# First FFN: plain fp32 products on unsplit weights for token tile 0, and the first block by token tile

## The chip, the cores and the metric

The kernel runs on one core of a Trainium2 chip. The metric is the device time of one execution in microseconds. The time before the change is 914.63 us, the median of three runs (914.24 to 914.75). The profile comes from a fourth execution, which took 913.31 us; its span, from the first to the last instruction, is 911.5 us.

## The reference

A decoder trunk with two layers on 256 tokens of width 1024, everything in float32. Around each attention stand two half-step SwiGLU FFNs with an inner width of 2816. The part that the change touches is the first FFN of the first layer:

```
h = h + 0.5 * swiglu(rms_norm(h, ffn1_norm[0]), ffn1_w_in[0], ffn1_w_out[0])

def swiglu(x, w_in, w_out):
    gate, up = split(x @ w_in, 2)        # w_in: 1024 x 5632
    return (silu(gate) * up) @ w_out     # w_out: 2816 x 1024
```

## The kernel before, in words

The 256 tokens are two tiles of 128 (t = 0 and 1). The contraction over 1024 is eight k of 128. TensorE (PE) multiplies a 128x128 piece of the transposed activations, which it holds, with a 128x512 piece of the weights, which streams through, into one PSUM bank of 512 columns.

**Split operands.** Nearly every product is made of three: each fp32 operand is split in two fp32r numbers, a rounded one (hi) and the rest (lo), and a step (`step`, L423) adds hi·hi, lo·hi and hi·lo into the bank. The weights arrive by DMA as fp32 in tiles called raw (1 MB, four k of 512 columns). ScalarE (ACT) casts a raw tile to w_hi (L404) and VectorE (DVE) subtracts to get w_lo (L406), in two pieces of 128x1024 per tile. The activations are split in the same way into one tile xT (written at L461 and L462).

**The first FFN's input.** x comes in four DMAs of 128x512 (hN). PE transposes each (L455, four 128x128 matrices into one bank), DVE multiplies the bank by the norm's gain in place (L1342), ACT casts and DVE subtracts. The factor of the root mean square is applied later, in the silu and in the product with up.

**The first block.** The FFN's 2816 columns are worked off in blocks. The first is a plain one of 512 columns (`plain`): two raw tiles of gate columns (i = 0 and 1, four k each) and two of up columns. Before the change it runs gate first, then up, and in each of them i = 0 for both token tiles and then i = 1 for both. So each w pair is used in one stretch and is free again. Its raw tiles come in four DMAs of 256 KB each. The next block is a narrow one of 256 columns, then come blocks with Strassen's seven products, and each block's part of the product with w_out lies between.

**What sets the order.** The code adds tasks with an assumed duration and a priority to a planner (`Plan`), which simulates the five engines and writes each engine's instructions in the order that comes out. So a change of constants or of tasks at the start can move everything behind it. Ahead of its first useful work PE runs products on a constant (tile warm, `warm_up`), whose result nobody reads; WARM sets how many.

**Buffers.** There are five raw tiles and five pairs of w tiles. A DMA for a raw tile stands in SP's queue until its predecessor in the same buffer has been split.

Of the kernel before, what the change touches and what calls it, by code (L numbers as in the profile page):

```python
# [44 lines left out]
FSUMS = 5000.0  # L45
TM = 1000.0
BOOST = 10000.0
C11 = True
RES = (True, True, True, True)
RES_SB = False  # L50
# [9 lines left out]


SB_ORDER = (("p", 0), ("s", 0), ("p", 1), ("v",), ("o", 0), ("s", 1), ("p", 2), ("o", 1), ("s", 2), ("p", 3), ("o", 2), ("s", 3), ("o", 3))
WARM = 14
NEWACC = False
QROT = False
ZQ = {(1, 0): 6, (2, 0): 7, (1, 1): 3}
# [2 lines left out]
EARLY = 300.0  # L69
X1 = 35  # L70
WAITM = 0
POSX = (-20000.0, -6000.0)
POSR = (-3000.0, -2000.0)
QORD = (('q', 0, 1), ('q', 0, 0), ('q', 1, 0), ('q', 2, 0), ('h', 0, 0), ('h', 0, 1), ('q', 1, 1), ('h', 1, 0), ('h', 1, 1), ('q', 2, 1), ('h', 2, 0), ('q', 3, 0), ('h', 2, 1), ('q', 3, 1), ('h', 3, 0), ('h', 3, 1))
OORD = [(0, range(6), (0, 1)), (1, range(6), (1,)), (0, range(6, 8), (0, 1)), (1, range(6, 8), (1,)), (1, range(8), (0,))]
# [20 lines left out]
class Buf:  # L96

    def __init__(self, make, base=()):
        self.make, self.base, self.ap_, self.all = make, list(base), None, []
        self.w, self.r = {}, {}  # L100
        self.slot = None
        self.by_halves = False

    @property
    def ap(self):
# [117 lines left out]
def kernel(  # L223
# [151 lines left out]
    def load(parts, a, b, cut=2):  # L375
        raw = RAW.get([P, a, b], F32, "raw")
        for sl, src in parts:
            ks = [(raw, i) for i in range(2)]
            if cut == 2 or len(parts) > 1:
                dma(src, lambda sl=sl: raw.ap[:, :, sl], P * a * (sl.stop - sl.start) * 4, ks, plan.pos - LOADS)  # L380
            else:
                for c in range(0, a, a // cut):
                    dma(src[:, c:c + a // cut], lambda c=c: raw.ap[:, c:c + a // cut], P * (a // cut) * b * 4,
                        [(raw, c)], plan.pos + 10 * c - 8.5e5)
        raw.ab, raw.cut = (a, b), cut
        return raw

    def flat(buf):
        return buf.ap.rearrange("p a b -> p (a b)")
# [3 lines left out]
    def split(raw, prio=None):  # L393
        prio = plan.pos - LEAD if prio is None else prio
        a, b = raw.ab
        hi, lo = WP.get([P, a, b], F32R, "w_hi"), WP.get([P, a, b], F32R, "w_lo")
        m = a * b // PIECES
        for j in range(PIECES):
            sl = slice(j * m, (j + 1) * m)
            ks = [j] if PIECES == 2 else [0, 1]  # L400
            rs = [2 * j, 2 * j + 1] if raw.cut == 4 else ks

            first = [(xh, (0, 0))] if raw.cut == 4 and j == 1 else []
            T("ACT", act(m), lambda sl=sl: ACT.copy(out=flat(hi)[:, sl], in_=flat(raw)[:, sl]),  # L404
              r=[(raw, i) for i in rs] + first, w=[(hi, i) for i in ks], prio=prio)
            T("DVE", dve(m), lambda sl=sl: DVE.tensor_sub(out=flat(lo)[:, sl], in0=flat(raw)[:, sl],  # L406
                                                          in1=flat(hi)[:, sl].bitcast(F32)),
              r=[(raw, i) for i in rs] + [(hi, i) for i in ks], w=[(lo, i) for i in ks], prio=prio)
        return hi, lo

    def weight(parts, a, b, cut=2, keep=False):
# [11 lines left out]
    def step(bank, w, kk, xk, first, last, cols_=every, piece=None):  # L423
        (sh, sl), keys = xk
        hi, lo = w
        piece = kk // 2 if piece is None else piece

        def run():
            r_h, r_l = hi.ap[:, kk, cols_], lo.ap[:, kk, cols_]
            mm(bank.ap, sh(), r_h, first, False)  # L430
            mm(bank.ap, sl(), r_h, False, False)
            mm(bank.ap, sh(), r_l, False, last)

        dense(3 * mmr(512), run, r=[(hi, piece), (lo, piece)] + keys, w=B(bank))

    def of_x(t, k):
        return ((lambda: xh.ap[:, k, ts(t)], lambda: xl.ap[:, k, ts(t)]), [(xh, (t, k // 4)), (xl, (t, k // 4))])
# [154 lines left out]
    def ffn(w_in, w_out, acc, rest, finish, kv=None, blocks=BLOCKS, roots=None, ending=False, there=False, arranged=False):  # L592
# [57 lines left out]
        def plain(n, c, by_t, cut=2):  # L650
# [29 lines left out]
            if by_t:  # L680
                for t in range(NT):
                    b = bank_()
                    for i in range(2):
                        gate(t, i, b)
                        if t == 1:
                            WP.put(*gw[i])
                    after_gate(t, b)
                    b = bank_()
                    for i in range(2):
                        up(t, i, b)  # L690
                        if t == 1:
                            WP.put(*uw[i])
                    after_up(t, b)
            else:
                for f, ws, fin in ((gate, gw, after_gate), (up, uw, after_up)):
                    bs = [bank_() for _ in range(NT)]
                    for i in range(2):
                        for t in range(NT):
                            f(t, i, bs[t])
                            if i == 1:  # L700
                                fin(t, bs[t])
                        WP.put(*ws[i])
# [134 lines left out]
        for n, kind in enumerate(blocks):  # L837
            if kind == "s":
                outs[n] = strassen(n, cols_[n], lambda: out(n - 1) if 0 < n < last else None)
            elif kind == "p":  # L840
                outs[n] = plain(n, cols_[n], n == 0 and not first, 4 if first and n == 0 else 2)
            else:
                outs[n] = narrow(n, cols_[n], n == 0 and not first)
            if n == last - 1:
# [492 lines left out]
    T("ACT", 60, lambda: nc.scalar.dma_start(out=gin, in_=ffn1_norm[0].rearrange("(j p k) -> p j k", j=2, k=4)), w=B(gc), prio=-9.5e5, lat=2500.0)  # L1337


    def first_operand(t, j, bank):  # L1340
        transposes(bank, lambda: [hN.ap[:, t, half(j)].rearrange("p (q k) -> p k q", k=4)[:, k, :] for k in range(4)], [(hN, (t, j))])
        T("DVE", dve(512), lambda: DVE.tensor_mul(  # L1342
            out=quarters(bank), in0=quarters(bank), in1=gin[:, j].unsqueeze(2).to_broadcast([P, 4, P])), r=B(gc), w=B(bank))
        part_to(bank, (xh, (t, j), lambda: xh.ap[:, 4 * j:4 * j + 4, ts(t)]), (xl, (t, j), lambda: xl.ap[:, 4 * j:4 * j + 4, ts(t)]), 512,
# [191 lines left out]
```

## Time and profile before

| what | value |
|---|---|
| median of three runs | 914.63 us |
| the profiled execution | 913.31 us |
| its span | 911.5 us |
| PE busy | 899.3 us (99%) |
| DVE busy | 818.2 us (90%) |
| ACT busy | 649.6 us (71%) |
| DMA | 214.44 MB, 235 GB/s in the mean |
| the chain that ended last | PE 81%, DVE 15% |

The page lists what each engine was busy with; the chain of waits goes back from the last instruction to whatever released it. A line of the kernel in these rows can be that of a helper: L283 is every product, L404 and L406 are every weight split. In the rows of the timeline the first number is the start and the second the time to the end of the last of the xN instructions. Matmuls overlap in these records (a 128x512 fp32r product is shown with some 390 ns, and follows its predecessor after 227 ns), so their cost is read from the starts.

### The profile page before, as it was taken

To read this page: it belongs to the slowest core of one execution; us is meant where nothing else is said; L and a number is where in the kernel's file an instruction comes from. 1 tells how busy PE (TensorE), PEld (TensorE's weight loads), DVE (VectorE), ACT (ScalarE), POOL (GpSimd) and SP (SyncE) were. 2 spreads that over 40 slices of the span, in tenths; PEclk is the share of its full clock that TensorE was granted. 3 is DMA by queue.
4 is the path that set the end of the run, shared out by engine and by line. 5 is a ranking of instruction groups with operands and counts; after the bars stand their busy time and mean duration, and the time that the engine had idled before them with its cause. 6 is when DMAs were issued, how large, how long until landed. Compare 5 with 4: busy or idle time off the path is not lost.

```text
span 911.5 us, 11855 instructions
## 1 busy us (share of the span) xinstructions
PE 899.3 (99%) x4446; PEld 743.7 (82%) x4446; DVE 818.2 (90%) x981; ACT 649.6 (71%) x925; POOL 65.5 (7%) x71
## 2 busy tenths in 40 slices
PE   9999999999999999999999999999999999999997
PEld 7888888888888878888888878888897777888886
DVE  7989999787967999999969999999689799999986
ACT  6857668677986865876778767667867677686663
POOL 1010101000000100110000101010000001010100
PEclk9999999999999999999999999999999999999999
DMA  9887999996853499999884999899853349998971
GB/s 335 311 203 216 306 268 242 311 246 186 264 184 126 106 260 284 236 280 303 251 269 135 251 279 276 256 326 234 298 180 116 94 94 273 293 258 268 335 209 47
DMA packets 107306, 214.44 MB, mean 235 GB/s; under 512 B 6256, under 2 KB 27760, under 8 KB 107248
## 3 DMA queue, kind: packets, MB, share of 16 engines
q1 hardware_dynamic: 85184, 170.49, 52.3%
q0 software_dynamic: 21648, 42.99, 27.2%
q8 instruction: 35, 0.57, 0.2%
q10 hardware_dynamic: 416, 0.20, 0.1%
q14 instruction: 23, 0.19, 0.1%
HBM read 212.62 MB, written 1.05 MB: 234 GB/s over the span
## 4 chain that ended last, share of the span: by engine, by line
PE 81%; DVE 15%; issue 2%; ACT 2%; POOL 0%; DVEq 0%; POOLq 0%; ACTq 0%
PE ps L283 77%; DVE w_lo L406 6%; PE ps L641 2%; DVE raw L575 1%; PE ps L455 1%; ACT w_hi L404 1%; DVE S_l L545 1%; DVE s L551 1%; DVE xT L462 1%; DVE w_lo L1115 1%; PE ps L1281 0%; DVE xs L1379 0%; DVE hN L532 0%; DVE aT_l L462 0%; DVE e L1273 0%
## 5 line engine op out<-in xcount | busy, mean ns | idle before, releaser
L406 DVE TENSOR_TENSOR w_lo<-raw,w_hi 128x1024 fp32r<-128x1024 f32 x432 | 509.3, 1221 | 30.3 <-ACT w_hi L404 28.5
L404 ACT CAST w_hi<-raw 128x1024 fp32r<-128x1024 f32 x432 | 430.1, 1050 | 96.7 <-DVE raw L575 41.1
L283 PE MATMUL ps<-w_hi,xT 128*128 128x512 f32 (+1 forms) x800 | 233.3, 375 | 0.0
L283 PEld LDWEIGHTS ps<-w_hi,xT 128*128 128x128 f32 x800 | 144.7, 188 | 25.9 <-DVE xT L462 0.2
L283 PE MATMUL ps<-w_lo,xT 128*128 128x512 f32 (+1 forms) x400 | 149.2, 373 | 0.3 <-DVE w_lo L406 0.3
L283 PE MATMUL ps<-w_hi,aT_h 128*128 128x512 f32 x354 | 139.9, 395 | 0.0
L283 PE MATMUL ps<-w_lo,aT_h 128*128 128x512 f32 x354 | 137.7, 389 | 0.0
L283 PE MATMUL ps<-w_hi,aT_l 128*128 128x512 f32 x354 | 137.5, 388 | 0.0
L283 PE MATMUL ps<-w_hi,S_h 128*128 128x512 f32 x320 | 126.9, 396 | 1.5 <-ACT p L735 1.5
L283 PE MATMUL ps<-w_lo,S_h 128*128 128x512 f32 x320 | 124.9, 390 | 0.3 <-DVE w_lo L406 0.3
L283 PE MATMUL ps<-w_hi,S_l 128*128 128x512 f32 x320 | 124.7, 390 | 0.0
L575 DVE TENSOR_TENSOR raw<-raw 128x1024 f32<-128x1024 f32 x78 | 93.7, 1221 | 0.2
L283 PEld LDWEIGHTS ps<-w_lo,xT 128*128 128x128 f32 x400 | 75.3, 188 | 14.4 <-DVE w_lo L406 1.1
L580 POOL DMA_DIRECT2D raw<-in_ffn_w_in_dram x38 | 48.1, 1267 | 516.8 <-DVE w_lo L406 218.0
L283 PEld LDWEIGHTS ps<-w_lo,aT_h 128*128 128x128 f32 x354 | 66.5, 188 | 13.9
L283 PEld LDWEIGHTS ps<-w_hi,aT_l 128*128 128x128 f32 x354 | 66.6, 188 | 12.9
L283 PEld LDWEIGHTS ps<-w_hi,aT_h 128*128 128x128 f32 x354 | 66.5, 188 | 12.8
L283 PEld LDWEIGHTS ps<-w_hi,S_h 128*128 128x128 f32 x320 | 60.1, 188 | 15.3 <-ACT p L735 3.0
L283 PEld LDWEIGHTS ps<-w_lo,S_h 128*128 128x128 f32 x320 | 60.1, 188 | 13.5 <-DVE w_lo L406 0.7
L283 PEld LDWEIGHTS ps<-w_hi,S_l 128*128 128x128 f32 x320 | 60.2, 188 | 11.6
L461 ACT CAST aT_h<-ps 128x512 fp32r<-128x512 f32 (+1 forms) x48 | 26.4, 549 | 55.1 <-PE ps L641 53.6
L283 PE MATMUL ps<-xT,w_hi 128*128 128x512 f32 (+1 forms) x136 | 46.8, 393 | 0.0
(176 smaller groups left out, 918.5 us busy)
## 6 DMA issues: line engine op xcount, KB each, us to landing
raw<-in_ffn_w_in_dram SPq DMA_DIRECT2D x76, 1024.0 KB, 7.8
raw<-in_ffn_w_out_dram SPq DMA_DIRECT2D x44, 1024.0 KB, 6.6
raw<-in_ffn_w_in_dram POOLq DMA_DIRECT2D x38, 1024.0 KB, 9.6
raw<-in_sb_w_qkv_dram SPq DMA_DIRECT2D x12, 1024.0 KB, 9.4
raw<-in_ffn_w_in_dram SPq DMA_DIRECT2D x16, 512.0 KB, 6.7
raw<-in_ffn_w_in_dram SPq DMA_DIRECT2D x16, 256.0 KB, 5.4
raw<-in_sb_w_o_dram SPq DMA_DIRECT2D x4, 1024.0 KB, 5.2
raw<-in_swa_w_q_dram SPq DMA_DIRECT2D x4, 1024.0 KB, 9.3
```

Source lines behind the costliest of these rows:

```text
L283: PE.matmul(ps, lhsT=lhsT, rhs=rhs, start=start, stop=stop, skip_group_check=True)
L404: T("ACT", act(m), lambda sl=sl: ACT.copy(out=flat(hi)[:, sl], in_=flat(raw)[:, sl]), r=[(raw, i) for i in rs] + first, w=[(hi, i) for i i ...
L406: T("DVE", dve(m), lambda sl=sl: DVE.tensor_sub(out=flat(lo)[:, sl], in0=flat(raw)[:, sl], in1=flat(hi)[:, sl].bitcast(F32)), r=[(raw, i) ...
L455: PE.matmul(bank.ap[:, i * P:(i + 1) * P], lhsT=s, rhs=ident, start=i == 0, stop=True, is_transpose=True, skip_group_check=True)
L461: T("ACT", act(n), lambda: ACT.copy(out=hi[2](), in_=src()), r=B(bank), w=[hi[0:2]])
L462: T("DVE", dve(n), lambda: DVE.tensor_sub(out=lo[2](), in0=src(), in1=hi[2]().bitcast(F32)), r=B(bank) + [hi[0:2]], w=[lo[0:2]])
L545: T("DVE", dve(512), lambda: DVE.tensor_sub(out=SL.ap[:, i].rearrange("p a b -> p (a b)"), in0=b.ap, in1=SH.ap[:, i].rearrange("p a b -> p ...
L551: T("DVE", dve(512), lambda: DVE.scalar_tensor_tensor(out=dst.ap, in0=x_.ap, scalar=sign, in1=y_.ap, op0=ALU.mult, op1=ALU.subtract), r=B( ...
L575: T("DVE", dve(m), lambda sl=sl: DVE.tensor_add(out=flat(dst)[:, sl], in0=flat(dst)[:, sl], in1=flat(src)[:, sl]), r=[(src, k) for k in ks ...
L580: T("POOL", 1500, lambda: nc.gpsimd.dma_start(out=dst.ap, in_=src, accum_op=ALU.add), w=[(dst, 0), (dst, 1)], prio=plan.pos - LOADS, lat=5 ...
L641: PE.transpose(out=tr.ap[:, i * P:(i + 1) * P], in_=m.ap[:, i * P:(i + 1) * P], identity=ident)
L1115: T("DVE", dve(512), lambda k=k, g_=g_: DVE.scalar_tensor_tensor(out=lo.ap[:, k], in0=raw.ap[:, k], scalar=g_(), in1=hi.ap[:, k].bitcast(F ...
```

## The change

Four edits meet in the first block of the first FFN.

1. **Plain products.** For token tile 0, the first six of the eight k of the gate columns are multiplied as fp32 with fp32, straight from the raw tile and from an unsplit copy of the activations (x_f), one product in place of three (`direct`). The other two k, and all of up, go on as split steps. Since token tile 1 still uses the split gate weights, all of the four raw tiles are split as before.
2. **By token tile.** The first block runs all of tile 0 (gate, then up), and then all of tile 1. The w pairs of the block are held until tile 1 has used them.
3. **Splits piece by piece.** The block's raw tiles are split in four pieces of 128x512 (one k, which is one DMA) rather than in two of 128x1024; a step waits for the piece of its own k. FINES and AFTER leave it at four pieces for each of the four tiles, and no piece waits for the first operand any more.
4. **x_f and fewer warm products.** For tile 0 DVE writes gain times transposed x to x_f in SBUF; ACT casts and DVE subtracts from there, and ACT copies x_f back into the bank (prio 0), where later sums read it. WARM goes from 14 to 9, that is from 40 products on the constant to 20. The planner's position for tile 1's operands (POSX) goes from -6000 to 0.

```diff
+DIRECT = 6
+FINES = (4,4,4,4)
+AFTER = 4
+FIRST_T = True
-WARM = 14
+WARM = 9
-POSX = (-20000.0, -6000.0)
+POSX = (-20000.0,0.0)
...
         raw.ab, raw.cut = (a, b), cut
+        raw.fine, raw.after = 2, {}
+        if cut == 4:
+            raw.fine = FINES[fines[0]]
+            if fines[0] == 0:
+                raw.after = {k: [(xh, (0, 0))] for k in range(AFTER, 4)}
+            fines[0] += 1
         return raw
...
+    def split_fine(raw, prio):
+        a, b = raw.ab
+        hi, lo = WP.get([P, a, b], F32R, "w_hi"), WP.get([P, a, b], F32R, "w_lo")
+        n = a // raw.fine
+        for c in range(0, a, n):
+            ks, at_ = range(c, c + n), [(buf, k) for buf in (hi,) for k in range(c, c + n)]
+            sl = slice(c * b, (c + n) * b)
+            T("ACT", act(n * b), lambda sl=sl: ACT.copy(out=flat(hi)[:, sl], in_=flat(raw)[:, sl]),
+              r=[(raw, k) for k in ks] + raw.after.get(c, []), w=[(hi, k) for k in ks], prio=prio)
+            T("DVE", dve(n * b), lambda sl=sl: DVE.tensor_sub(out=flat(lo)[:, sl], in0=flat(raw)[:, sl],
+                                                              in1=flat(hi)[:, sl].bitcast(F32)),
+              r=[(raw, k) for k in ks] + [(hi, k) for k in ks], w=[(lo, k) for k in ks], prio=prio)
+        hi.fine = lo.fine = True
+        return hi, lo
...
-        piece = kk // 2 if piece is None else piece
+        piece = kk if hi.fine else kk // 2 if piece is None else piece
...
+    def direct(bank, raw, kk, xf, first, last):
+        def run():
+            mm(bank.ap, xf.ap[:, kk], raw.ap[:, kk], first, last)
+
+        dense(4 * 512 / 2.4 + 20, run, r=[(raw, kk), (xf, 0)], w=B(bank))
...
                     for i in range(2):
+                        if first and t == 0 and 4 * i < DIRECT:
+                            raw = load([(slice(0, 512), col(0, i, c))], 4, 512, cut)
+                            gw[i] = split(raw)
+                            for kk in range(4):
+                                if 4 * i + kk < DIRECT:
+                                    direct(b, raw, kk, plainly[i], i == kk == 0, i == 1 and kk == 3)
+                                else:
+                                    step(b, gw[i], kk, of_x(0, 4 * i + kk), i == kk == 0, i == 1 and kk == 3)
+                            RAW.put(raw)
+                            STG.put(plainly[i])
+                            continue
                         gate(t, i, b)
...
-                outs[n] = plain(n, cols_[n], n == 0 and not first, 4 if first and n == 0 else 2)
+                outs[n] = plain(n, cols_[n], n == 0 and (FIRST_T or not first), 4 if first and n == 0 else 2)
...
+        if t == 0 and 4 * j < DIRECT:
+            plainly[j] = xf = STG.get([P, 4, P], F32, "x_f")
+            T("DVE", dve(512), lambda: DVE.tensor_mul(
+                out=xf.ap, in0=quarters(bank), in1=gin[:, j].unsqueeze(2).to_broadcast([P, 4, P])), r=B(gc, bank), w=B(xf))
+            T("ACT", act(512), lambda: ACT.copy(out=xh.ap[:, 4 * j:4 * j + 4, ts(t)], in_=xf.ap), r=B(xf), w=[(xh, (t, j))])
+            T("DVE", dve(512), lambda: DVE.tensor_sub(out=xl.ap[:, 4 * j:4 * j + 4, ts(t)], in0=xf.ap, in1=xh.ap[:, 4 * j:4 * j + 4, ts(t)].bitcast(F32)),
+              r=B(xf) + [(xh, (t, j))], w=[(xl, (t, j))])
+            copy_act(lambda: quarters(bank), lambda: xf.ap, 512, B(xf), B(bank), prio=0.0)
+            return
```

What the planner makes of it is shown at three places. Rows read: line, operation, what it writes <- what it reads, shape, count. Buffer numbers tell tiles apart. Lines of the changed kernel are its own (L287 is the product that was L283, L490 the transposes that were L455, L434 the lo pieces of the first block).

**PE, from the last warm product on.** Before (raw tile 0 of gate is w_hi_178 and w_lo_202):

```order
L283 LDWEIGHTS warm_71
L283 MATMUL ps_66<-warm_71 128x256
L455 MATMUL ps_66<-ident_68,hN_63 128x128 x4
L283 MATMUL ps_66<-w_hi_178,xT_158 128x512 x2
L283 MATMUL ps_66<-w_lo_202,xT_158 128x512
L455 MATMUL ps_66<-ident_68,hN_63 128x128 x4
L283 MATMUL ps_66<-w_hi_178,xT_158 128x512 x2
```

And now (raw_113 and raw_185 are gate's two raw tiles; w_170 and w_176 are the split of the first, w_216 and w_222 that of the second):

```order
L287 MATMUL ps_66<-warm_71 128x256
L287 MATMUL ps_66<-raw_113,x_f_152 128x512 x4
L490 MATMUL ps_66<-ident_68,hN_63 128x128 x4
...
L490 MATMUL ps_66<-ident_68,hN_63 128x128 x4
L287 MATMUL ps_66<-raw_185,x_f_167 128x512 x2
L287 MATMUL ps_66<-w_hi_170,xT_163 128x512 x2
L287 MATMUL ps_66<-w_lo_176,xT_163 128x512
```

Before, 26 warm products stand between the second transpose group of tile 0 and the first of tile 1. Now four stand there, then four plain products come, then tile 1's first transposes, two warm products (left out above), its second transposes, two plain products, three steps of token tile 1 on the first gate tile, the two split steps of gate's last k, and then up for tile 0 and the 13 steps that are left of tile 1.

**DVE, the stretch in which the first block's lo pieces are made.** Before:

```order
L406 TENSOR_TENSOR w_lo_202<-raw_113,w_hi_178 128x1024 x2
L1342 TENSOR_TENSOR ps_66<-ps_66,gcols_81 128x512 x2
L484 SCALAR_TENSOR_TENSOR small_67<-small_67 128x1
L1420 TENSOR_SCALAR small_67<-small_67 128x1
L462 TENSOR_TENSOR xT_158<-ps_66,xT_158 128x4x128
L1420 TENSOR_SCALAR small_67<-small_67 128x1
L406 TENSOR_TENSOR w_lo_249<-raw_197,w_hi_234 128x1024
```

And now, from the last lo piece of the first gate tile on:

```order
L434 TENSOR_TENSOR w_lo_176<-raw_113,w_hi_170 128x512
L1399 TENSOR_TENSOR ps_66<-ps_66,gcols_81 128x512
L343 CAST mask_win_76<-mw1_f_154 128x128
L1399 TENSOR_TENSOR ps_66<-ps_66,gcols_81 128x512
L497 TENSOR_TENSOR xT_163<-ps_66,xT_163 128x4x128
L434 TENSOR_TENSOR w_lo_222<-raw_185,w_hi_216 128x512
L497 TENSOR_TENSOR xT_163<-ps_66,xT_163 128x4x128
L434 TENSOR_TENSOR w_lo_222<-raw_185,w_hi_216 128x512 x3
L434 TENSOR_TENSOR w_lo_252<-raw_214,w_hi_240 128x512 x4
```

Tile 1's operands (the two gain products and the two lo parts) stand between the pieces of the first and of the second gate tile, as before; each of them waits for PE's transposes of tile 1, which now stand behind four plain products.

**SP, the loads behind the second gate tile.** Before (raw_225 and raw_255 are up's tiles, raw_268 and raw_290 the narrow block's, raw_316 is w_out):

```order
L364 DMA raw_225<-in_ffn1_w_in_dram 128x512 x4
L364 DMA raw_255<-in_ffn1_w_in_dram 128x512 x2
L364 DMA raw_268<-in_ffn1_w_in_dram 128x4x256
L364 DMA raw_255<-in_ffn1_w_in_dram 128x512 x2
L364 DMA raw_290<-in_ffn1_w_in_dram 128x4x256
L364 DMA raw_268<-in_ffn1_w_in_dram 128x4x256
L364 DMA raw_316<-in_ffn1_w_out_dram 128x2x1024
```

And now (raw_214 and raw_237 are up's tiles, raw_267 and raw_287 the narrow block's, raw_299 is w_out):

```order
L368 DMA raw_214<-in_ffn1_w_in_dram 128x512 x4
L368 DMA raw_237<-in_ffn1_w_in_dram 128x512 x4
L368 DMA raw_267<-in_ffn1_w_in_dram 128x4x256
L368 DMA raw_287<-in_ffn1_w_in_dram 128x4x256
L368 DMA raw_299<-in_ffn1_w_out_dram 128x2x1024
L368 DMA raw_267<-in_ffn1_w_in_dram 128x4x256
```

Up's last two pieces stand ahead of the narrow block's first half now, and w_out's first tile ahead of the narrow block's second halves. From the first sum of weights of the first Strassen block (L575 before, L610 now) on, all five engines have the same instructions in the same order as before.

More of the change, by code (lines that the diff above doesn't have):

```diff
@@ L101, in __init__ @@
         self.slot = None
-        self.by_halves = False
+        self.by_halves = self.fine = False
     @property
@@ L385, in load @@
         raw.ab, raw.cut = (a, b), cut
+        raw.fine, raw.after = 2, {}
[4 more added lines that the diff above has]
+            fines[0] += 1
         return raw
+    fines = [0]
     def flat(buf):
@@ L395, in split @@
         a, b = raw.ab
+        if raw.cut == 4:
+            return split_fine(raw, prio)
         hi, lo = WP.get([P, a, b], F32R, "w_hi"), WP.get([P, a, b], F32R, "w_lo")
@@ L1337 @@
     T("ACT", 60, lambda: nc.scalar.dma_start(out=gin, in_=ffn1_norm[0].rearrange("(j p k) -> p j k", j=2, k=4)), w=B(gc), prio=-9.5e5, lat=2500.0)
+    plainly = {}
     def first_operand(t, j, bank):
         transposes(bank, lambda: [hN.ap[:, t, half(j)].rearrange("p (q k) -> p k q", k=4)[:, k, :] for k in range(4)], [(hN, (t, j))])
+        if t == 0 and 4 * j < DIRECT:
[7 more added lines that the diff above has]
+            return
         T("DVE", dve(512), lambda: DVE.tensor_mul(
```

## The prediction

> **What bounds the kernel now.** First the page: its busy times (part 1) and the chain that ended last (part 4).
>
> ```profile
> PE 899.3 (99%) x4446; PEld 743.7 (82%) x4446; DVE 818.2 (90%) x981; ACT 649.6 (71%) x925; POOL 65.5 (7%) x71
> PE 81%; DVE 15%; issue 2%; ACT 2%; POOL 0%; DVEq 0%; POOLq 0%; ACTq 0%
> ```
>
> PE is the bound nearly everywhere, so the change pays only by what PE does in vain. Next the chain of waits of the first 60 us (start, length, what), and PE's timeline there.
>
> ```profile
> 0.93 2.75 PE ps L283 x12
> ...
> 6.03 3.25 PE ps L283 x26
> 9.28 0.48 PE ps L455 x4
> 9.76 0.70 PE ps L283 x3
> 10.46 0.47 PE ps L455 x4
> 10.93 21.17 PE ps L283 x93
> 32.09 0.44 PE ps L641 x4
> ```
>
> ```profile
> 4.54 0.64 PE L283 MATMUL ps<-warm 128*128 128x256 bf16 x2
> 4.96 1.06 PE L455 MATMUL ps<-ident,hN 128*128 128x128 f32 x4
> 5.82 3.46 PE L283 MATMUL ps<-warm 128*128 128x256 bf16 x26
> 9.12 0.64 PE L455 MATMUL ps<-ident,hN 128*128 128x128 f32 x4
> ...
> 31.93 0.27 PE L641 MATMUL ps<-ident,m 128*128 128x128 f32 x1
> ```
>
> Useful work without a break begins at 9.12. From there to the first turn of the block's result at 31.93 PE issues the 32 steps of the first block and two transpose groups, 22.81 us. The 93 products in 21.17 us are 31 steps of 0.683 us; 32 of them are 21.86, which leaves 0.95 for the two groups. Third, whether a gain at the start reaches the end: busy time by stretches (stretch, its length, then PE, PEld, DVE, ACT, POOL, the clock, DMA).
>
> ```profile
> 9.10:32.10 23.00, 23.00 (x108) 19.05 (x107) 18.96 (x22) 17.09 (x23) 0.55 (x1) 1.00 1.06 385
> 45.00:100.00 55.00, 55.00 (x252) 45.46 (x250) 50.29 (x51) 36.52 (x44) 4.97 (x4) 1.00 0.83 218
> 100.00:200.00 100.00, 100.00 (x482) 83.53 (x481) 88.32 (x94) 72.61 (x93) 8.51 (x8) 1.00 0.94 276
> 200.00:290.00 90.00, 90.00 (x540) 75.24 (x540) 70.09 (x94) 71.53 (x110) 1.26 (x1) 1.00 0.62 187
> ```
>
> PE has no gap up to 290 us, while DVE is idle for 5 to 20 us of each stretch: the splits run ahead of PE. So PE may come about a microsecond earlier without finding an empty buffer, and everything behind shifts by the same amount.
>
> **The start moves.** Before, 26 warm products stand ahead of tile 1's transposes at 9.12. Now four stand ahead of the first plain product. What one costs depends on the clock. The clock column of the stretches shows 1.00 from the first microsecond on, but the same product shows otherwise (count, ns min/median/max; up to 6.4 us, and from 6.5 on):
>
> ```profile
> L283 PE MATMUL ps<-warm x17: 397/421/421, 0.9 to 6.2; 128*128 128x256 bf16 x17
> L283 PE MATMUL ps<-warm x23: 273/275/354, 6.5 to 9.0; 128*128 128x256 bf16 x23
> ```
>
> The two at 4.54 follow each other in 0.21 us (0.42 to the next row); a late one takes half of it, 0.11. With four at 0.21 PE reaches the first plain product at 5.82 + 0.85 = 6.67, just when the clock opens. It needs x_f, which DVE makes in the place of the first gain product, and the first 256 KB of gate weights:
>
> ```profile
> 4.78 0.70 DVE L1342 TENSOR_TENSOR ps<-ps,gcols 128x512 f32<-128x512 f32 x1 [1.68 <-PE ps L455]
> 6.06 0.70 DVE L1342 TENSOR_TENSOR ps<-ps,gcols 128x512 f32<-128x512 f32 x1 [0.46 <-PE ps L455]
> L364 SPq DMA_DIRECT2D raw<-in_ffn_w_in_dram x4: 424/432/432, 1.7 to 3.1; - x4
> DMA to landing us min/median/max: 3.4/3.8/4.1
> ```
>
> x_f is there at 5.5 and 6.8, the four pieces between 5.1 and 7.2, so PE is the last. Useful work starts at 6.67 in place of 9.12: minus 2.45 us. Two warm products are left between the transpose groups of tile 1: plus 0.22.
>
> **The plain product.** It replaces three passes of 227 ns, 0.683 us. The trace has no fp32 product of 128x512; the nearest are the attention scores, four fp32 products that run in pairs, in their second passes:
>
> ```profile
> 672.16 0.92 PE L283 MATMUL ps<-kT_s,qT 64*128 64x256 f32 x8
> L283 PE MATMUL ps<-kT_s,qT x2: 376/376/376, 672.5 to 672.5; 64*128 64x256 f32 x2
> L283 PE MATMUL ps<-kT_s,qT x4: 269/270/272, 672.7 to 672.8; 64*128 64x128 f32 x4
> ```
>
> Four products in the code are eight records, so an fp32 product is two passes. 128 columns more cost 376 - 270 = 106 ns per pass: 512 columns are 0.43, two passes 0.86 us. Bounds: at the 227 ns per pass of a split step 0.455; by the whole group, 0.86 us for 384 columns of a pair in two passes, 1.15. I take 0.86. Six cost 6 x (0.86 - 0.683) = plus 1.06, or between -1.4 and +2.8 by the bounds; and in that group the second passes start 0.3 us after the first, 0.1 more than a pass of 256 columns takes, so the first of a row of plain products costs plus 0.1. The sum is 2.45 - 0.22 - 1.06 - 0.1 = 1.07 us saved.
>
> **Can the splits keep up?** By tile, PE uses up four weight tiles in the time that it had for two, and the pieces have to come at the pace of a step, 0.683 us.
>
> ```profile
> 6.67 0.68 DVE L462 TENSOR_TENSOR xT<-ps,xT 128x512 fp32r<-128x512 f32 x1
> 7.27 0.15 DVE L484 SCALAR_TENSOR_TENSOR small<-small 128x1 f32<-128x1 f32 x1
> 10.88 1.29 DVE L1342 TENSOR_TENSOR ps<-ps,gcols 128x512 f32<-128x512 f32 x2
> 14.92 4.62 DVE L406 TENSOR_TENSOR w_lo<-raw,w_hi 128x1024 fp32r<-128x1024 f32 x4
> 35.92 0.69 DVE L545 TENSOR_TENSOR S_l<-s,S_h 128x512 fp32r<-128x512 f32 x1
> 36.65 0.69 DVE L551 SCALAR_TENSOR_TENSOR s<-s,ps 128x512 f32<-128x512 f32 x1
> 11.61 0.59 ACT L461 CAST xT<-ps 128x512 fp32r<-128x512 f32 x1 [0.96 <-DVE ps L1342]
> 12.09 1.05 ACT L404 CAST w_hi<-raw 128x1024 fp32r<-128x1024 f32 x1
> ```
>
> A 1024 piece costs DVE 1.155; one of 512 follows after 0.60 (6.67 to 7.27), at worst after 0.73 (35.92 to 36.65). ACT takes 0.48 and isn't the limit, also with its two copies of x_f more. PE: plain products to 10.2, transposes, at 11.4 the fifth and sixth, at 13.1 the three steps of tile 1, at 15.15 gate's last two k; the last needs its lo piece at 16.3. DVE: the first transposes are visible at 10.85, two gain products to 12.3, xl after ACT's cast to 13.0, then four pieces and one xl to 16.05. PE would find it 0.1 us ago, and from there DVE gains 0.08 per step. I charge nothing, but the cover is thin: each 0.1 us more per DVE instruction is half a microsecond.
>
> The page "VectorE: DVE Perf Modes" of the Trainium skill (The TRN2 errata) speaks against small pieces: an SBUF operation pays a fixed latency, and an fp32 tensor_tensor takes (N+151)/0.96 ns, 0.69 us for 512. The rows agree on the length; by it as the pace, an estimate is 0.35 us of waiting, and the sum would be 0.7 saved.
>
> **Weights.** The transfers behind the first four (issued at 4.5 and 12.6, and to landing), and w_out's first use:
>
> ```profile
> L364 SPq DMA_DIRECT2D raw<-in_ffn_w_in_dram x1: 431/431/431, 4.5 to 4.5; - x1
> DMA to landing us min/median/max: 5.4/5.4/5.4
> L364 SPq DMA_DIRECT2D raw<-in_ffn_w_in_dram x1: 424/424/424, 12.6 to 12.6; - x1
> DMA to landing us min/median/max: 6.3/6.3/6.3
> 43.75 0.39 PE L283 MATMUL ps<-w_hi,aT_h 128*128 128x512 f32 x1
> ```
>
> The fifth piece lands at 9.9, PE wants it at 11.4. Up's last lands at 18.9 before; now the narrow block's 512 KB no longer stand ahead of it, at 385 GB/s 1.4 us sooner, 17.5, and DVE reaches it near 20. The narrow block's last halves go behind w_out's first 1 MB (2.7 us): SP waits for gate's second buffer until 16, so they land by 25.5, and are first used after 31. Nothing to charge. The longer hold of the w pairs is covered too: the next block finds the fifth pair free, and w_out's tile, which waits for the first, isn't needed before some 42.7 us (43.75 less the gain).
>
> The sum against the profiled execution is 913.31 - 1.07 = 912.24; that run stands 1.32 below the median of the three, and against this **914.63 - 1.07 = 913.56, I say 913.6**. From 913.1 to 914.3 I call it this case (chance 0.5). What a measurement of this kernel can tell from no change is about 0.2%, 1.83 us, so this case is "same".
>
> **Rival: DVE sets the pace (0.2).** With 0.73 per instruction gate's last lo piece comes at 16.65, visible at 16.8, 0.5 late, and up's eight pieces lose 0.05 each: 0.9 us, 914.5. For it: the order puts tile 1's operands ahead of the pieces. Against it: the 512 rows at 6.67 and at 10.88 (1.29 for two) follow faster.
>
> **Rival: the clock opens earlier (0.15).** The opening at 6.7 is 5.7 us after PE's first product. Were it at 4.5, PE would be free by 5.6, 1.07 sooner; DVE, which has six instructions of 0.6 after 6.76, comes free at 10.4 in place of 10.85, so 0.5 of that is lost to a wait for the lo piece: 0.6 more saved, 913.0. Against it: one execution, one opening. The page "TensorE: Matmul & The Clock Gate" of the Trainium skill (Part 1) says that the gate opens after a busy window of 3.4 us which runs freely; the 5.7 us here fit, and an estimate is an opening anywhere between 4.3 and 7.8 us.
>
> **Rival: slower, by plain products at half clock (0.05).** Fewer warm products, and if the clock stays closed behind 6.67, a plain product costs 1.71. Each microsecond later loses half a one; from 8.8 on the gain is gone, and with all six at half clock (5.1 us) it is 1.07 - 5.1 = 4 us slower, 918.7. Against it: PE does the same things up to 6.67, and it goes on without a gap.
>
> **Rival: the head isn't the bound (0.1).** If a later stretch waits for DVE or a load whatever PE does, the time stays at 914.6. For it: 15% of the chain is DVE. Against it: the rows to 290 us.
>
> **How the numbers follow.** Under 912.80 is faster: half of the early clock (0.08), a product near the 0.455 bound (0.04), a part of the forecast whose covers prove thicker (0.08), 0.2 in all. Over 916.46 is slower: half clock, 0.05. The rest, 0.75, is same. The range, 912.3 to 915.3, reaches up to a product of 1.15 us (1.74 more, 915.3) and down to an early clock with cheaper products.
>
> **What would show it.** PE's first plain product at 6.6 to 6.8 us; twelve records of raw,x_f, 0.43 apart; the first turn of m for tile 0 at about 24 us and PE's first step of the narrow block near 31.3; no PE wait for w_lo over 0.3 us before that; the same distances from there on. The prediction is wrong if the products follow each other after over 1 us, if PE stands between 13 and 22 us, or if a shift seen at 45 us is gone at 290.

## The result, and the profile after

| | before | after |
|---|---|---|
| median, first comparison (12 executions each) | 914.69 us (913.57 to 915.57) | 911.95 us (911.29 to 914.04) |
| ratio, 95% interval | | 0.9974 (0.9965 to 0.9982) |
| median, second comparison (33 and 11 executions) | 913.91 us | 911.85 us |
| ratio, 95% interval | | 0.9980 (0.9972 to 0.9989) |
| the profiled execution | 913.31 us | 911.76 us |
| its span | 911.5 us | 909.9 us |

By the ratios the change saves 2.4 us in the first comparison (1.6 to 3.2 by the interval) and 1.8 in the second (1.0 to 2.6). Of all the executions that were timed one, with twelve warm products (below), took 1255.36 us at a granted clock of 0.669, and its ratio leaves it out. The forecast was 913.6, a saving of 1.07 and by the bound of 0.2% no change. The time came 0.35 us below the range, and the saving lies at that bound or a little beyond it: the case to which I had given a chance of 0.2.

The page of the changed kernel, busy times and the shares of the chain of waits:

```profile
PE 897.6 (99%) x4420; PEld 739.5 (81%) x4420; DVE 818.7 (90%) x989; ACT 650.4 (71%) x935; POOL 68.4 (8%) x71
PE 81%; DVE 14%; issue 2%; ACT 2%; POOL 1%; POOLq 0%; DVEq 0%; ACTq 0%
```

PE is the bound as before, with 26 records fewer. PE's timeline of the changed kernel (start, time to the end of the last, what, count):

```profile
4.04 0.72 PE L490 MATMUL ps<-ident,hN 128*128 128x128 f32 x4 [0.36 <-POOL mw_f L341]
4.59 0.38 PE L287 MATMUL ps<-warm 128*128 128x256 bf16 x2
4.82 0.64 PE L490 MATMUL ps<-ident,hN 128*128 128x128 f32 x4
5.29 0.61 PE L287 MATMUL ps<-warm 128*128 128x256 bf16 x4
5.86 3.67 PE L287 MATMUL ps<-raw,x_f 128*128 128x512 f32 x8
9.37 0.63 PE L490 MATMUL ps<-ident,hN 128*128 128x128 f32 x4
9.84 0.38 PE L287 MATMUL ps<-warm 128*128 128x256 bf16 x2
10.06 0.64 PE L490 MATMUL ps<-ident,hN 128*128 128x128 f32 x4
10.54 1.88 PE L287 MATMUL ps<-raw,x_f 128*128 128x512 f32 x4
11.86 1.05 PE L287 MATMUL ps<-w_hi,xT 128*128 128x512 f32 x2
23.25 0.60 PE L676 MATMUL ps<-ident,m 128*128 128x128 f32 x4
30.52 0.61 PE L287 MATMUL ps<-w_hi,xT 128*128 128x512 f32 x2
```

The last two rows are the first turn of m and the first step of the narrow block. The first plain product starts at 5.86, not at 6.67. The four transposes at 4.04 take 0.55 us up to the next row, where the group at 4.96 in the profile before took 0.86 (to 5.82): the clock is open here before the transposes, and was not there. Everything behind has the forecast's distances, 0.8 earlier: first turn 23.25 for 24, narrow block 30.52 for 31.3.

Does it reach the end? The chain of waits of the changed kernel, the rows that stand against 44.59, 340.75, 402.52 and 449.49 of the chain before:

```profile
42.72 0.22 PE ps L676 x2
...
339.06 0.47 PE ps L287 x2
...
400.75 12.96 PE ps L287 x57
...
447.72 12.28 PE ps L287 x54
```

```profile
44.59 0.22 PE ps L641 x2
...
340.75 0.47 PE ps L283 x2
...
402.52 12.95 PE ps L283 x57
...
449.49 10.93 PE ps L283 x48
```

PE's lead over the kernel before is 1.87 us at 45 us, 1.69 at 340, 1.77 at 400 and at 449, and 1.6 in the span. In what follows, "lead" is this: PE's rows of one execution matched in order with those of the profiled execution of before, at 45 us.

DVE's timeline of the changed kernel, and PE's waits in the first 60 us (us in total, times, longest):

```profile
12.27 0.68 DVE L434 TENSOR_TENSOR w_lo<-raw,w_hi 128x512 fp32r<-128x512 f32 x1
12.86 0.69 DVE L497 TENSOR_TENSOR xT<-ps,xT 128x512 fp32r<-128x512 f32 x1
13.46 4.30 DVE L434 TENSOR_TENSOR w_lo<-raw,w_hi 128x512 fp32r<-128x512 f32 x7
17.68 0.15 DVE L519 SCALAR_TENSOR_TENSOR small<-small 128x1 f32<-128x1 f32 x1
```

```profile
PEld ps L287 <- DMA raw<-in_ffn_w_in_dram: 1.3, 4, 0.5
PEld ps L287 <- DVE xT L497: 0.4, 1, 0.4
PEld ps L287 <- DVE w_lo L434: 0.2, 1, 0.2
```

Seven pieces take 17.68 - 13.46 = 4.22, so one follows another after 0.60 us, and PE waits for a lo piece once, for 0.2.

### The profile page after: what moved, and what is told of

Read it like the earlier page. It is cut to its first block, busy times and chain, and to the rows that moved or that the text cites. A ratio compares the mean times of both kernels' runs of the same rounds, so it can differ in the third digit from the quotient of the medians.

```text
span 909.9 us, 11824 instructions
## 1 busy us (share of the span) xinstructions
PE 897.6 (99%) x4420; PEld 739.5 (81%) x4420; DVE 818.7 (90%) x989; ACT 650.4 (71%) x935; POOL 68.4 (8%) x71
## 4 chain that ended last, share of the span: by engine, by line
PE 81%; DVE 14%; issue 2%; ACT 2%; POOL 1%; POOLq 0%; DVEq 0%; ACTq 0%
PE ps L287 78%; DVE w_lo L420 6%; PE ps L676 2%; DVE raw L610 1%; PE ps L490 1%; ACT w_hi L418 1%; DVE S_l L580 1%; DVE s L586 1%; DVE xT L497 1%; PE ps L1327 0%; DVE xs L1436 0%; DVE hN L567 0%; DVE e L1319 0%; DVE aT_l L497 0%; POOL small L522 0%
## 5 line engine op out<-in xcount | busy, mean ns | idle before, releaser
L420 DVE TENSOR_TENSOR w_lo<-raw,w_hi 128x1024 fp32r<-128x1024 f32 x424 | 499.4, 1220 | 29.1 <-ACT w_hi L418 27.5
L418 ACT CAST w_hi<-raw 128x1024 fp32r<-128x1024 f32 x424 | 422.1, 1050 | 99.3 <-DVE raw L610 41.1
L287 PE MATMUL ps<-w_hi,xT 128*128 128x512 f32 (+1 forms) x788 | 229.8, 376 | 0.0
L287 PEld LDWEIGHTS ps<-w_hi,xT 128*128 128x128 f32 x788 | 142.6, 188 | 26.0 <-DVE xT L497 0.4
L287 PE MATMUL ps<-w_lo,xT 128*128 128x512 f32 (+1 forms) x394 | 147.1, 373 | 0.2 <-DVE w_lo L420 0.2
L287 PE MATMUL ps<-w_hi,aT_h 128*128 128x512 f32 x354 | 139.9, 395 | 0.0
L287 PE MATMUL ps<-w_lo,aT_h 128*128 128x512 f32 x354 | 137.7, 389 | 0.0
L287 PE MATMUL ps<-w_hi,aT_l 128*128 128x512 f32 x354 | 137.4, 388 | 0.0
L287 PE MATMUL ps<-w_hi,S_h 128*128 128x512 f32 x320 | 126.9, 396 | 1.4 <-ACT p L781 1.4
L287 PE MATMUL ps<-w_lo,S_h 128*128 128x512 f32 x320 | 124.9, 390 | 0.3 <-DVE w_lo L420 0.3
L287 PE MATMUL ps<-w_hi,S_l 128*128 128x512 f32 x320 | 124.7, 390 | 0.0
L610 DVE TENSOR_TENSOR raw<-raw 128x1024 f32<-128x1024 f32 x78 | 93.6, 1219 | 0.3
L287 PEld LDWEIGHTS ps<-w_lo,xT 128*128 128x128 f32 x394 | 74.1, 188 | 14.6 <-DVE w_lo L420 1.4
L287 PEld LDWEIGHTS ps<-w_lo,aT_h 128*128 128x128 f32 x354 | 66.5, 188 | 14.0
L287 PEld LDWEIGHTS ps<-w_hi,aT_l 128*128 128x128 f32 x354 | 66.6, 188 | 12.9
L287 PEld LDWEIGHTS ps<-w_hi,aT_h 128*128 128x128 f32 x354 | 66.5, 188 | 12.8
L287 PEld LDWEIGHTS ps<-w_hi,S_h 128*128 128x128 f32 x320 | 60.1, 188 | 15.2 <-ACT p L781 2.9
L287 PEld LDWEIGHTS ps<-w_lo,S_h 128*128 128x128 f32 x320 | 60.1, 188 | 13.5 <-DVE w_lo L420 0.7
L287 PEld LDWEIGHTS ps<-w_hi,S_l 128*128 128x128 f32 x320 | 60.2, 188 | 11.7
L287 PE MATMUL ps<-xT,w_hi 128*128 128x512 f32 (+1 forms) x136 | 47.0, 394 | 0.0
```

What stands on the lines that cost most here:

```text
L287: PE.matmul(ps, lhsT=lhsT, rhs=rhs, start=start, stop=stop, skip_group_check=True)
L610: T("DVE", dve(m), lambda sl=sl: DVE.tensor_add(out=flat(dst)[:, sl], in0=flat(dst)[:, sl], in1=flat(src)[:, sl]), r=[(src, k) for k in ks ...
```

## The experiments

All are whole programs that compute everything. WARM sets the number of products on the constant (20 for the 9 of the changed kernel, 40 for the 14 before, 12 for 7, none for 4), DIRECT the plain ones, FINES the pieces of each split, FIRST_T the order by token tile. They fall into three comparisons, each with the kernel before beside it on the same chip; its medians there were 914.42, 913.83 and 913.91, so across them the ratios compare and the medians don't.

**The same two kernels again.** No edit: one more profile of the kernel before and one of the changed kernel, and later the changed kernel in a timed comparison.

> The kernel before once more, unchanged, for a second profile of its head. Theory A (the clock's opening sets the head): first step of the block at 9.5 us whenever the clock opens before about 6.7 us, because the first lo piece is ready only at 9.8; if it opens later, up to 0.6 us later; the time stays between 913.3 and 915.0. Rival (the head is the same, and what varies is spread over the whole run): the first turn of the block's result at 31.9 as before, and a time that differs from 913.3 by what stretches behind 45 us lose.

> The changed kernel once more, unchanged. Theory A: the first plain product starts at 5.9 us if the clock is open before the transposes of tile 0, and at 6.7 if it opens behind them; the first turn follows 17.4 to 17.7 us behind that start, and the time moves with it, 911.8 to 912.6. Rival (the start has little to do with the time): a start at 5.9 or 6.7 and a time that doesn't follow it.

> The changed kernel unchanged, beside the three above on one chip. Theory: the head makes it 1.8 us shorter than the kernel before, in the fastest executions of both as in the median (911.3 against 913.1); what goes beyond in a median is how many executions lose time behind 390 us. So 911.9 to 912.2, ratio 0.9975 to 0.9985. Rival (the 2.4 of the first comparison is the change's own): ratio 0.9974 or less again, with the fastest executions 2.4 apart.

The pace of the transposes and of the constant's products tells when the clock opens. The third profile of the changed kernel, PE's timeline and its chain of waits:

```profile
3.92 1.10 PE L490 MATMUL ps<-ident,hN 128*128 128x128 f32 x4 [0.24 <-POOL mw_f L341]
4.81 0.64 PE L287 MATMUL ps<-warm 128*128 128x256 bf16 x2
5.24 1.05 PE L490 MATMUL ps<-ident,hN 128*128 128x128 f32 x4
6.09 0.64 PE L287 MATMUL ps<-warm 128*128 128x256 bf16 x4
6.57 3.60 PE L287 MATMUL ps<-raw,x_f 128*128 128x512 f32 x8
10.00 0.63 PE L490 MATMUL ps<-ident,hN 128*128 128x128 f32 x4
23.83 0.60 PE L676 MATMUL ps<-ident,m 128*128 128x128 f32 x4
```

```profile
43.29 0.22 PE ps L676 x2
```

| execution | clock opens | first plain product | first turn | lead |
|---|---|---|---|---|
| before, profiled | 6.6 us | | 31.93 | |
| before again | 5.2 | | 32.03 | -0.1 |
| changed, profiled | 3.6 to 4.0 | 5.86 | 23.25 | 1.88 |
| changed again | 4.0 | 5.71 | 23.36 | 1.77 |
| changed, third | 6.1 | 6.57 | 23.83 | 1.30 |

With the late clock (4.81 to 5.24 for two products on the constant, 0.215 each) the changed kernel does what was forecast: first plain product 6.57 for 6.67, and 0.1 us earlier than that is a lead of 1.07 + 0.1 = 1.17, against 1.30 measured. With the early one it starts 0.7 to 0.9 earlier. The kernel before got nothing from its early clock. From its second profile, PE's timeline:

```profile
5.70 3.07 PE L283 MATMUL ps<-warm 128*128 128x256 bf16 x26
9.18 0.75 PE L455 MATMUL ps<-ident,hN 128*128 128x128 f32 x4 [0.41 <-DMA hN<-in_x_dram]
```

The 26 products on the constant end at 8.77, half a microsecond earlier than with the late clock (5.82 + 3.46 = 9.28), but then PE stands for 0.41 us until tile 1's x has landed, and the transposes start at 9.18 (9.12 with the late clock); the first step comes at 9.68, where I had expected 9.5. The changed kernel's first useful products need only tile 0's x and the first weights, so it profits from an early clock. In the third profile eight plain passes take 10.00 - 6.57 = 3.43, 0.429 each.

The timed comparison gave 0.9980, as the theory had it, and the shortest executions are 911.24 and 913.08, 1.84 apart, the lead of an early clock. The 2.4 of the first comparison isn't the change's size in every comparison; 1.8 lies in both intervals.

**Warm products as before.**

```diff
-WARM = 9
+WARM = 14
```

> The changed kernel with 40 warm products in place of 20: six more stand among the head's transposes and plain products, and 14 behind gate's first steps, where PE would have useful work. Theory A (PE is the bound from the first plain product on): each warm product behind that start costs its 0.11 us, so plus 2.2 us, 914.2, about the time before. Rival (the splits bound the head, PE has slack there): less than 0.8 us more, 912.7.

```profile
10.13 0.63 PE L490 MATMUL ps<-ident,hN 128*128 128x128 f32 x4
10.60 0.61 PE L287 MATMUL ps<-warm 128*128 128x256 bf16 x4
11.04 0.64 PE L490 MATMUL ps<-ident,hN 128*128 128x128 f32 x4
11.52 0.61 PE L287 MATMUL ps<-warm 128*128 128x256 bf16 x4
...
25.98 1.74 PE L287 MATMUL ps<-warm 128*128 128x256 bf16 x14
```

In PE's timeline (above) the order puts the additional products where PE has work: six in the head (4 + 4 for 2 in these rows), and fourteen behind 25.98, which cost 27.47 - 25.98 = 1.49 us. Median 914.8, ratio 1.0003 (0.9993 to 1.0013); the clock opened late, at 6.5. The whole gain is gone, as Theory A had it: PE is the bound in the head, and the products hide behind nothing there.

**No warm products.**

```diff
-WARM = 9
+WARM = 4
```

> The changed kernel with no product on the constant at all, so that PE's first work is tile 0's transposes near 3.7 us. It prices the rival 'plain products at half clock' of the prediction: records of raw,x_f 0.86 us apart until the clock opens, 0.43 behind. Between 3 and 6 us after PE's first work the clock opened in the runs so far, so here at 6.5 to 9.5: one to four records at half clock, 0.4 to 1.7 us lost, 912.3 to 913.6. If the transposes and products with gaps don't count as busy for the clock, all twelve are slow: 917. If the warm products aren't needed at all: 911.9 or less.

PE's timeline, and its records on x_f up to 8.6 us (ns min/median/max):

```profile
3.70 2.00 PE L490 MATMUL ps<-ident,hN 128*128 128x128 f32 x8 [3.70 <-DMA hN<-in_x_dram]
5.59 5.17 PE L287 MATMUL ps<-raw,x_f 128*128 128x512 f32 x8
24.67 0.60 PE L676 MATMUL ps<-ident,m 128*128 128x128 f32 x4
```

```profile
L287 PE MATMUL ps<-raw,x_f x4: 737/1061/1222, 5.6 to 8.3; 128*128 128x512 f32 x4
```

The second, third and fourth record start at 6.60, 7.455 and 8.31: 0.854 us per pass, a plain product of 1.71, as the slower rival priced it. The clock opens 4.8 us after PE's first work (at 8.5), three passes and a part are slow, and the first turn comes at 24.67, 1.4 late. Lead 0.44; 913.02, ratio 0.9992 (0.9983 to 1.0001). Even with no warm-up at all the change isn't slower than before.

**Twelve warm products, none later.** `WARM = 9` becomes `WARM = 7`.

> The changed kernel with 7 for the warm products: the twelve at the start stay, the two between tile 0's transposes, the four ahead of the first plain product and the two between tile 1's are gone. Theory A: x_f is ready 0.2 to 0.4 us sooner, so the first plain product starts near 5.5 in place of 5.8; of the 0.22 behind it tile 1's operands (0.4 us wait) give back most. About 911.6, 0.3 under the changed kernel (which was 911.95 and 912.03). Rival: the first plain product waits for the weights' DMA and the first split step for tile 1's xT whatever PE does: 911.95. Rival: with fewer products the clock opens later; each 0.5 us of half clock costs 0.25: 912.2 or more.

The first plain product starts at 5.46, the first turn is at 23.17, 0.08 us earlier than in the changed kernel. Lead 1.96, median 911.96, ratio 0.9978 (0.9968 to 0.9987). What PE saves in the head it spends waiting: between 8 and 14 us its weight loads wait 0.6 for tile 1's x, 0.4 for its xT and 0.3 for weights, and its second split step starts at 12.88, 0.1 before that of the changed kernel (12.98), though the plain products began 0.4 before. So the plain products start where Theory A had them, but the time is that of the rival, and from here on transfers and operands set the pace, as it says.

**The parts alone.** Four programs without plain products (DIRECT = 0) and with 9 for the warm products:

```diff
# the kernel before, fewer warm products: halves, both token tiles in turn
-WARM = 14
+WARM = 9
# fine pieces, both token tiles in turn
-DIRECT = 6
-FIRST_T = True
+DIRECT = 0
+FIRST_T = False
# halves, by token tile
-DIRECT = 6
-FINES = (4,4,4,4)
+DIRECT = 0
+FINES = (2,2,2,2)
# fine pieces, by token tile (the changed kernel without plain products)
-DIRECT = 6
+DIRECT = 0
```

> The kernel before, with 9 in place of 14 for the warm products (20 on the constant in place of 40) and nothing else. Theory A (the time goes by when PE's work without gaps begins, and by how much work is left then): tile 1's transposes come right behind the first two steps, the first w_lo piece of 128x1024 is there near 8 us, the third step starts at 9.5 to 10 in place of 11.46; 1.5 to 2 us saved, about 912.7 against the before of the same call (914.4), PE's first turn near 30.2 in place of 31.93. Rival B (before's 26 warm products only fill a hole that the coarse pieces leave; tile order, pieces and plain products are what gains): under 0.6 us saved, 913.9 or more.

> The changed kernel without the plain products and without the order by token tile: pieces of one k, 9 for the warm products and the position 0 for tile 1's operands stay. Theory A: PE is fed from 5.9 on as it was in the run without plain products; about 912.7, within 0.4 of that run. If the order by token tile is what gained there: 914 or more. If pieces and fewer warm products are worth the more the fewer pieces PE needs per microsecond (gate first uses each piece for both tiles): under 912.3.

> The changed kernel without the plain products and with the splits in halves of two k as before; order by token tile, 9 for the warm products and the position 0 stay. With it the four corners stand beside each other: coarse by pair (no gain measured), fine by pair (no gain measured), fine by token tile (1.5 us measured), and this, coarse by token tile. If the order by token tile carries the gain by itself: 912.7. If what counts is that PE has something to do while the first splits are made, by token tile it uses a piece for one tile only and runs out sooner with coarse pieces: a hole of over 1 us ahead of 14 us, 914.0 or more.

> The change without plain products (all products split), the rest kept: by token tile, pieces of one k, 20 warm products. Theory A: the first step waits for the first lo piece and starts near 7.3 us, 1.4 later than the plain product, saves 1.05 for the six dearer products, and then waits some 1 us for the second gate tile's lo pieces; 912.9, about 1 us slower than the changed kernel. Rival (finer pieces alone carry the gain): 911.9, the same as the changed kernel. Rival (the plain products alone carry it): 914.5, the time before.

| | median | ratio (95%) | lead |
|---|---|---|---|
| halves, in turn | 914.19 | 1.0001 (0.9993 to 1.0010) | -0.2 |
| halves, by token tile | 914.50 | 1.0009 (1.0000 to 1.0018) | 0.0 |
| fine, in turn | 913.53 | 1.0000 (0.9991 to 1.0009) | 1.4 |
| fine, by token tile | 912.73 | 0.9984 (0.9975 to 0.9993) | 0.8 |
| the same with six plain products | 911.85 | 0.9980 (0.9972 to 0.9989) | 1.3 to 1.9 |

My expectation for the first (1.5 to 2 us saved) was wrong. Its timeline of PE:

```profile
7.03 0.75 PE L455 MATMUL ps<-ident,hN 128*128 128x128 f32 x4 [1.37 <-DMA hN<-in_x_dram]
...
11.91 0.50 PE L283 MATMUL ps<-w_hi,xT 128*128 128x512 f32 x1
13.08 0.50 PE L283 MATMUL ps<-w_hi,xT 128*128 128x512 f32 x1 [0.66 <-DVE xT L462]
```

And of DVE:

```profile
9.40 1.23 DVE L406 TENSOR_TENSOR w_lo<-raw,w_hi 128x1024 fp32r<-128x1024 f32 x1 [0.41 <-ACT w_hi L404]
...
12.34 0.68 DVE L462 TENSOR_TENSOR xT<-ps,xT 128x512 fp32r<-128x512 f32 x1
```

PE begins its first step at 7.54, two microseconds earlier than before (9.52), and loses them again: the two products of the step at 11.91 stand 1.17 apart, because the second needs tile 1's last lo operand, which DVE ends at 13.02. Ahead of it on DVE stands a piece of 128x1024, which itself had to wait for ACT's cast of 128x1024 and lets the next instruction start at 10.55, and then the four instructions on tile 1's operands. With halves by token tile PE has the same hole (11.77 to 12.93), as expected. So I take it that time which PE is given at the start is worth something only if DVE gets the operands through in time, and there the fine pieces count: with them the lead is 0.8 and 1.4.

These four programs don't isolate the pieces, though, because the planner also moves the four loads of x among those of the weights. The load of tile 0's second half goes out second before and in the changed kernel, third in the two programs with fine pieces and fourth in the two with halves; PE waits 1.37 us for it in the first (the row at 7.03). The first program also keeps the planner's position of before (POSX), and the other three have the new one. What the coarse pieces cost and what the later load costs isn't separated.

Against the run without plain products, the six plain products fill holes: that run does four split steps between 5.85 and 12.08, and the changed kernel six k between 5.86 and 12.26. Two k are 1.37 us, less the 0.18 between the ends 1.2, and the leads differ by 1.88 - 0.80 = 1.08. But the holes there are waits for x: the planner puts tile 1's loads of x behind more of the weights, and PE's transposes of it wait for them for 1.2 us in two groups. So the 1.08 is what the plain products and the order of the loads are worth together. I had expected that run's first step near 7.3, and it started at 5.85; its time came as expected (912.9 forecast). By the times the step from none to six plain products isn't settled, since the two intervals overlap.

The order by token tile alone didn't show a gain of its own in the head (0.0 against -0.2, 0.8 against 1.4). In the times "fine, in turn" came out worse than its lead and than I had expected, 1.0000 for 1.4 us; this belongs to the part on what differs behind the head.

**How many plain products.** `DIRECT = 6` becomes 4, or 8.

> The changed kernel with four in place of six plain products: k 4 and 5 of tile 0's gate are split steps again. By PE's time alone 2 x 0.175 = 0.35 us would be saved (911.6). If the plain products are worth it because they need no split: the fifth piece lands near 10, its lo is there near 11.7, and PE, ready at 10.5, stands for about a microsecond before the step; first turn 0.3 to 0.8 later than 23.25, 912.3 to 912.8.

> The changed kernel with eight plain products, so all of tile 0's gate. By PE's time alone 2 x 0.175 = 0.35 us are lost (912.3). If they cover the 0.4 us that the first split step waits for, 911.9, first turn within 0.15 of 23.25.

The clock opened at 5.4 and 6.6, so the time from the first plain product to the first turn is compared: 17.64 us with four (6.12 to 23.76), 17.58 with eight (6.82 to 24.40), and with six 17.39, 17.65 and 17.26 in the three executions. Medians 913.03, ratio 0.9986 (0.9977 to 0.9995), and 912.94, 0.9988 (0.9978 to 0.9997), beside 911.85 for six. Both medians lie above what I had expected. Against the least disturbed execution with six (17.26) the head is 0.3 to 0.4 us longer: for eight that is the price of two more plain products in place of split steps (2 x 0.175 = 0.35), and there was no wait left to cover. Four compares less well, since the planner moves the loads of tile 1's x there too; its lead, 1.4, lies within the 1.3 to 1.9 of six, and that of eight is 0.7. The medians favour six, but the intervals overlap, so it isn't settled that six is best.

**Where executions differ behind the head.** Up to 330 us all the executions keep the lead that they have at 60 us, to within 0.2. Between 330 and 505 us some of them lose more: the execution with eight plain products 2.2 us, with four 2.1, fine pieces in turn 1.3, the third of the changed kernel 0.6; between the profiled ones of before and of the changed kernel nothing is lost. The chain of waits with eight plain products there, and the waits of ACT (345 to 405 us) and of PE's weight loads (345 to 480):

```profile
347.75 11.09 DMA raw<-in_ffn_w_in_dram
...
377.69 12.85 DMA raw<-in_ffn_w_in_dram
...
405.07 10.93 PE ps L287 x46
```

```profile
ACT w_hi L418 <- DMA raw<-in_ffn_w_in_dram: 9.5, 3, 4.6
```

```profile
PEld ps L490 <- ACT hN L565: 1.4, 1, 1.4
PEld ps L287 <- DVE w_lo L420: 1.0, 2, 0.6
```

In the profiled execution of the changed kernel the chain is on PE from 338 to 461 us, and ACT's waits in the same stretch read:

```profile
ACT w_hi L418 <- DMA raw<-in_ffn_w_in_dram: 6.6, 2, 3.4
```

I take it that the weights' transfers and PE are nearly level here, and that where a piece comes late, PE waits for what ACT and DVE make of it. Over all fourteen profiled executions: ACT waited 8.2 to 9.5 us for these transfers in eight, of which seven lost 0.6 to 2.2 us against the kernel before's first profile and one 0.1 (the kernel before again). It waited 6.1 to 7.7 in six, of which five lost 0.2 at most, but one, warm products as before, lost 1.4 with a wait of 7.3. So the losses go with the transfers, but these are not shown to be the whole cause. PE has the same instructions in the same order behind 50 us in all of these programs. What decides how often it happens stays open: the median lies 0.4 us above the shortest execution for fine pieces by token tile, 0.6 for the changed kernel, 1.2 for fine pieces in turn and 0.8 to 1.4 for the kernel before, with 11 to 33 executions each. That would explain why the first of these has a better time than its lead and the third a worse one, but one to three profiles per program do not show it.

## Why the prediction was right or wrong

**The start (minus 2.45): the mechanism held, the size did not.** "With four at 0.21 PE reaches the first plain product at 6.67": it was 5.86, 5.71 and 6.57 in three executions. The step took the opening of the clock in one execution, 6.6 us, for the kernel's. The term measures 9.12 - 5.86 = 3.26 with an early clock (the first plain product's weight load had waited 0.2 us there, so PE was no longer the last) and 2.55 with a late one. 1.07 + 0.81 = 1.88 is the lead that was measured, so this term holds the error in the head. (The 0.1 that was charged for the first of a row and didn't come went into two small waits, 0.08 among the first eight passes and 0.04 at the first split step, both below.)

**The clock opens earlier (a rival with 0.15, 913.0).** This is what happened in the comparison's profile. I had let half of it be lost to a wait for gate's last lo piece. That wait was 0.2 for PE's weight load, and the wait for tile 1's xT, 0.4, hardly shows in PE: the plain products end at 10.54 + 4 x 0.429 = 12.26 and the second split step starts at 12.98, 0.04 later than a step of 0.683 would. The page "TensorE: Matmul & The Clock Gate" of the Trainium skill (Part 1) says that the busy window runs freely, so the opening moves from run to run. The thirteen profiled executions with warm products agree with that: by the pace of their records the clock opened between about 3.6 and 6.6 us, 2.7 to 5.7 behind PE's first product at 0.93. The lower end lies under the 4.3 that I had estimated from the page's 3.4 us. The rival deserved the better part of the forecast's chance.

**The plain product (plus 1.06, plus 0.1).** 0.858 us against the 0.86 worked out from the attention scores; the 0.1 for the first of a row isn't there (eight passes in 3.43).

**The two warm products (plus 0.22).** 9.84 to 10.06: 0.22.

**DVE (charged nothing).** Right: 0.60 per piece. The rival with 0.73 per instruction (0.2, 914.5) is out. The page "VectorE: DVE Perf Modes" of the Trainium skill (The TRN2 errata) gives 0.69 us for a piece, and the rows show this as the length (0.68 and 0.69), but they follow each other after 0.60; with the length as the pace the prediction's estimate was 0.35 us of waiting.

**The weights (charged nothing).** Right for a late start. With PE there at 5.86, its weight loads wait for transfers four times (1.3 us in sum, 0.2 in the third execution), most of it behind running products: the eight passes take 9.37 - 5.86 = 3.51 where they need 3.43. From the start at 5.71 in the second execution they take 9.36 - 5.71 = 3.65, so an earlier start is in part given back to the transfers.

**Half clock (0.05, 918.7).** Priced rightly, 1.71 per product, but too severe in its case: even with no warm product only three and a half of twelve passes are slow.

**The head isn't the bound (0.1).** Between the two compared profiles the lead holds to the end (1.87, then 1.6), as forecast. But the prediction rested on the rows to 290 us, and behind them lies a stretch in which the profiled executions lose between 0 and 2.2 us.

**The chances.** I measured the profiled execution's saving against a median of three, and left the executions' own spread (913.1 to 917.4 for the kernel before over all comparisons) out of the range: the low end, 912.3, was an early clock with half its gain given back, and cheaper products.

## What to carry to other kernels

Time that is freed at the start of a program is worth something only as far as the operands arrive: fewer warm products alone gave nothing here, because PE then stood waiting for x and for DVE's operands. With fine pieces PE was 0.8 and 1.4 us ahead in the head, and with plain products as well 1.3 to 1.9, in one to three profiles each; what each part is worth by itself isn't settled, since the programs without plain products also differ in the order of the loads. A time that is read from one profile and depends on the state of the clock is to be carried through a sum with both of its ends, since the same kernel started its first plain product at 5.7 and at 6.6 us. And a gain at the start is to be followed through every stretch to the last one: where transfers and PE are level, an execution can lose as much as the edit gained.

## What the runs showed of the hardware

- The clock opened about 2.7 to 5.7 us after PE's first product, in thirteen executions that begin alike (twelve products on a constant, then transposes). The plain products ran at the full clock with the warm products and, without them, at half of it for three and a half passes (0.854 us a pass against 0.429). The clock column of the stretches showed 1.00 throughout.
- An fp32 product of 128x512 is two passes of 0.429 us; eight passes in a row keep that pace while weights arrive and DVE splits them.
- A DVE tensor_tensor of 128x512 between SBUF tiles is 0.68 to 0.69 us long and follows its like after 0.60, in a row of seven (4.22 us).
